# A decoder's forgetting attention with its gates added by TensorE in paired heads, and operand tiles of 258 columns

## The chip, the cores and the metric

The kernel runs on one core of a Trainium2 chip. The metric is the time of one launch on the device, in microseconds (us); lower is better. The kernel before takes 1029.21 us (median of 3 runs, 1028.37 to 1030.59).

A core has five engines, which run their own instruction streams: PE (matrix products; its weight loads are listed apart as PEld), DVE (vector work), ACT (activations), POOL, and SP, which here issues the DMAs. PE reads from the on-chip memory SBUF and writes PSUM.

## The reference

Two blocks of a decoder over 256 tokens of width 1024. The first mixes with a recurrent branch, gated linear attention and a block-sparse attention (MoBA), and ends in a SwiGLU feed-forward. The second has a short convolution layer, and a layer of forgetting attention (FoX), each with a SwiGLU feed-forward of width 2816. What the change touches is FoX, with 16 heads of 64:

```python
log_f = jax.nn.log_sigmoid((h @ w_f + b_f).astype(jnp.float32))
log_fcum = jnp.cumsum(log_f, axis=1).transpose(0, 2, 1)          # F, one row of 256 per head
logits = jnp.einsum("bhqd,bhkd->bhqk", qb, kb)                   # query blocks of 128
logits = logits + log_fcum[:, :, q0:kend, None] - log_fcum[:, :, None, :kend]
logits = jnp.where(kpos[None, :] <= qpos[:, None], logits, -jnp.inf)
p = jax.nn.softmax(logits, axis=-1)
outs.append(jnp.einsum("bhqk,bhkd->bhqd", p, vb))                # then o @ w_o
```

All other products are plain matrix products: activations times weight matrices.

## The kernel before, in words

Activations lie transposed: 128 features on the partitions, 256 tokens in the columns, 8 such tiles for the width. Every large product is made of three passes in the reduced format fp32r: an operand a is kept as a high part and a rest (`hilo`, `hl_tiles`), and a*w is computed as ah*wh + ah*wl + al*wh (`mm3`, L150 to L152; `ksteps`, L185 to L191). So a 128x128 weight block costs three matmuls of 256 columns. Weights stream from HBM as 512 KB chunks of 8 blocks (`raw`); ACT makes the high part of a chunk (L139, `wh`), DVE the rest (L143, `wl`). Beside them DVE computes a matrix-vector product of the modulation in pieces (`gw`, L359), spread over the program by `fill`.

The operands of the products are in three kinds of tiles, named by what they carry: `xh`/`xl`, `yh`/`yl` (both from `hl_tiles`, L244) and `mh`/`ml` (the feed-forward's inner operand, in `ffn`). Tiles of x are T + 2 = 258 columns wide, because in some stages two more columns are used; y and m tiles have 256. A tile of 258 fp32 columns has 1032 bytes on each partition, one of 256 has 1024, and tiles of a pool lie behind one another. The products that this concerns read columns 0 to 255 in either case.

FoX comes after the convolution layer's feed-forward. K is projected (`wk`), the gates' small projection and the log-sigmoid make F, V is projected (`wv`), and then a loop over 8 pairs of heads does for pair i: the query projection (`single("wq", i)`, 24 matmuls), for each head two logits products in fp32 (L691, L694) with a causal mask added by two bf16 products (L693, L696), DVE's addition of a bias tile with a maximum (L699, L700), ACT's exponentials (L703, L704), the scaling (L706, L707), three transposes by PE into a `plg` tile (L716 to L718), ACT's copy (L720), two products with V (L721, L722), and a step of the output projection `wo` (12 matmuls in `ksteps`). The bias F[t] - F[s] is brought to the 128 partitions through memory: F is written to a scratch row (`f_scr`, L1159), each pair reads its two rows back to all partitions (`f_b`, L1181), and ACT makes the bias tiles (`m_b`, L1186, L1187) from them and from a transposed copy of F.

The order on each engine is set when the program is built: a scheduler walks through the program with modelled times and lays down each engine's stream, and the engines then run in that order and wait on semaphores. `after` adds an order between two instructions.

Of the kernel before, what the change touches and what calls it, by code (L numbers as in the profile page):

```python
# [14 lines left out]
ALU = mybir.AluOpType  # L15
# [21 lines left out]
WARM = (5, 3, 5, 0)  # L37
RSQ_SEED = 1595953144
# [24 lines left out]
class Net:  # L63
# [180 lines left out]
    def hl_tiles(self, tag, pool=None):  # L244

        w = T + 2 if tag == "x" else T
        h = self.tl(pool or self.xp, [P, w], tag + "h", F32R, NK)
        l = self.tl(pool or self.xp, [P, w], tag + "l", F32R, NK)
        return h, l, h[:, 0:T], l[:, 0:T]
# [128 lines left out]
    def consts(self):  # L378
# [21 lines left out]
        nc.scalar.activation(self.tbl, self.tbl, AF.Exp)  # L400
        self.identb = self.tl(cp, [P, P], "identb", BF16)
# [281 lines left out]
    def attn_p(self, q, k, hh, bias, mask=False):  # L683
# [7 lines left out]
        mm(lg[:, 0:256], q[r, 128:256], k[r, 0:256], start=True, stop=not mask)  # L691
        if mask:
            mm(lg[:, 128:256], self.identb, self.cmask, start=False, stop=True)  # L693
        mm(lg[:, 256:384], q[r, 0:128], k[r, 0:128], start=True, stop=not mask)  # L694
        if mask:
            mm(lg[:, 256:384], self.identb, self.cmask, start=False, stop=True)  # L696
# [27 lines left out]
    def attn_out(self, i, Ls, v):  # L724
# [4 lines left out]
        return self.hilo(pv, "y")  # L729

# [49 lines left out]
    def ffn(self, l, X, R=None, R2=None, first=(), rows=None):  # L780
# [5 lines left out]
        def evac(g, u):  # L786
# [12 lines left out]
            h = self.tl(self.fp, [P, T], "mh", F32R)  # L799
            lo = self.tl(self.fp, [P, T], "ml", F32R)  # L800
# [151 lines left out]
    def run(self):  # L952
# [193 lines left out]
        fz = self.small_proj(1, XK)  # L1146
        z = self.tmp("f_z", bufs=1)[:32]
        A.activation(z, fz, AF.Copy)
        fz = self.ms([16, T])
        nc.tensor.matmul(fz, self.fold, z, start=True, stop=True)  # L1150
        z = z[:16]
# [210 lines left out]
```

## Time and profile before

| | us |
|---|---|
| median of 3 runs | 1029.21 |
| the profiled execution's own time | 1030.16 |
| its span (first to last instruction) | 1028.4 |
| PE busy | 956.9 (93%) |
| DVE busy | 810.7 (79%) |
| ACT busy | 537.0 (52%) |
| POOL busy | 20.5 (2%) |
[...]

Times in rows are us from the span's start unless ns stands beside them. [...] "[7.42 <-DVE a_mx L700]" behind a row is the idle time of the engine before that instruction, and what ended it. [...] The FoX loop stands at 706 to 798 us.

### The profile page before, as it was taken

The numbers are of one execution on the slowest core, as the hardware profiler recorded it, in microseconds if no ns is written. First come the engines' busy times: TensorE is split into PE (matmuls) and PEld (weight loads), VectorE is DVE, ScalarE is ACT, GpSimd is POOL, SyncE is SP. The second block draws the span as 40 slices with busy tenths as digits, with TensorE's granted clock in tenths as the row PEclk, the third lists the DMA queues.
The fourth block names the chain that finished last, engine by engine and source line by source line (L and its number), as shares of the span: only waits on it lengthen the run. The fifth ranks groups of instructions, "written<-read, shape, count | busy, mean of one in ns | idle before, by whom it ended". The sixth has DMA issues, their size and how long they took to land.

```text
span 1028.4 us, 19193 instructions
## 1 busy us (share of the span) xinstructions
PE 956.9 (93%) x7384; PEld 913.4 (89%) x7384; DVE 810.7 (79%) x1635; ACT 537.0 (52%) x971; POOL 20.5 (2%) x65
## 2 busy tenths in 40 slices
PE   7979998999999799987899999998899889999996
PEld 7878988999999699987899999977587889999995
DVE  7897487999887888779999999797355898866554
ACT  7575454544443544546454444486556575544432
POOL 1210000000000000000000000000000000000001
PEclk9999998999999899998899999999699989999998
DMA  8753256888899577654799999647332457565641
GB/s 302 252 169 106 83 187 209 281 296 282 294 334 369 182 232 247 197 169 177 262 323 340 315 335 374 189 131 243 99 122 86 124 160 234 181 186 184 185 141 41
DMA packets 63532, 221.69 MB, mean 216 GB/s; under 512 B 7256, under 2 KB 8944, under 8 KB 63440
## 3 DMA queue, kind: packets, MB, share of 16 engines
q1 hardware_dynamic: 62240, 217.18, 63.3%
q0 software_dynamic: 1056, 3.16, 1.1%
q8 instruction: 58, 0.95, 0.4%
q14 instruction: 34, 0.28, 0.1%
q10 hardware_dynamic: 144, 0.13, 0.0%
HBM read 219.36 MB, written 2.65 MB: 216 GB/s over the span
## 4 chain that ended last, share of the span: by engine, by line
PE 81%; DVE 11%; ACT 3%; issue 3%; DMA 2%; DVEq 0%; ACTq 0%; SPq 0%
PE acc L150 19%; PE acc L151 19%; PE acc L152 19%; PE acc L185 4%; PE acc L186 4%; PE acc L191 4%; DVE wl L143 3%; DVE gw L359 2%; PE ms L721 1%; ACT wh L139 1%; DMA f_b<-f_scr 1%; PE lg L691 1%; PE acc L241 1%; PE acc L240 1%; PE acc L239 1%
## 5 line engine op out<-in xcount | busy, mean ns | idle before, releaser
L139 ACT ACTIVATE wh<-raw 128x1024 fp32r<-128x1024 f32 (+2 forms) x296 | 307.5, 1046 | 272.4 <-PE acc L152 134.9
L143 DVE TENSOR_TENSOR wl<-raw,wh 128x1024 fp32r<-128x1024 f32 (+2 forms) x296 | 356.3, 1206 | 92.1 <-ACT wh L139 89.6
L150 PE MATMUL acc<-yh,wh 128*128 128x256 f32 x608 | 172.2, 284 | 0.7 <-DVE ff_m L798 0.7
L151 PE MATMUL acc<-yh,wl 128*128 128x256 f32 x608 | 172.3, 284 | 0.0
L152 PE MATMUL acc<-yl,wh 128*128 128x256 f32 x608 | 172.1, 284 | 0.0
L150 PE MATMUL acc<-xh,wh 128*128 128x256 f32 x576 | 164.1, 285 | 5.8 <-DVE ff_u L791 4.1
L151 PE MATMUL acc<-xh,wl 128*128 128x256 f32 x576 | 163.6, 284 | 0.0
L152 PE MATMUL acc<-xl,wh 128*128 128x256 f32 x576 | 163.2, 283 | 0.0
L151 PE MATMUL acc<-mh,wl 128*128 128x256 f32 x528 | 149.3, 283 | 0.5 <-DVE wl L143 0.5
L152 PE MATMUL acc<-ml,wh 128*128 128x256 f32 x528 | 149.1, 283 | 0.0
L150 PE MATMUL acc<-mh,wh 128*128 128x256 f32 x528 | 148.8, 283 | 0.0
L359 DVE SCALAR_TENSOR_TENSOR gw<-gw,cact 128x1024 f32<-128x1024 f32 x112 | 135.1, 1218 | 4.4 <-DMA gw<-ada 4.3
L150 PEld LDWEIGHTS acc<-yh,wh 128*128 128x128 f32 x608 | 116.9, 193 | 0.8 <-issue 0.8
L151 PEld LDWEIGHTS acc<-yh,wl 128*128 128x128 f32 x608 | 116.9, 192 | 0.0
L152 PEld LDWEIGHTS acc<-yl,wh 128*128 128x128 f32 x608 | 116.9, 192 | 0.0
L150 PEld LDWEIGHTS acc<-xh,wh 128*128 128x128 f32 x576 | 110.2, 191 | 6.9 <-DVE ff_u L791 4.3
L151 PEld LDWEIGHTS acc<-xh,wl 128*128 128x128 f32 x576 | 110.4, 192 | 0.6 <-issue 0.5
L152 PEld LDWEIGHTS acc<-xl,wh 128*128 128x128 f32 x576 | 110.0, 191 | 0.0
L151 PEld LDWEIGHTS acc<-mh,wl 128*128 128x128 f32 x528 | 101.4, 192 | 0.7 <-DVE wl L143 0.7
L152 PEld LDWEIGHTS acc<-ml,wh 128*128 128x128 f32 x528 | 101.3, 192 | 0.0
L150 PEld LDWEIGHTS acc<-mh,wh 128*128 128x128 f32 x528 | 101.1, 192 | 0.0
L185 PE MATMUL acc<-xh,wh 128*128 128x256 f32 (+1 forms) x256 | 68.3, 294 | 7.6 <-ACT wh L139 5.5
(382 smaller groups left out, 1604.7 us busy)
## 6 DMA issues: line engine op xcount, KB each, us to landing
raw<-wts SPq DMA_DIRECT2D x288, 512.0 KB, 4.4
gw<-ada SPq DMA_DIRECT2D x112, 512.0 KB, 5.4
f_b<-f_scr SPq DMA_DIRECT2D x8, 256.0 KB, 3.4
raw<-wts SPq DMA_DIRECT2D x6, 256.0 KB, 5.5
m_scr<-m_row POOLq DMA_DIRECT2D x2, 768.0 KB, 6.1
ax<-xT SPq DMA_DIRECT2D x4, 256.0 KB, 5.0
m_b<-m_scr POOLq DMA_DIRECT2D x8, 128.0 KB, 3.4
out<-fg SPq DMA_DIRECT2D x8, 128.0 KB, 1.8
```

What stands on the lines that cost most here:

```text
L139: i = nc.scalar.activation(self.wh[:, d], r, AF.Copy)
L143: self.anchor = nc.vector.tensor_tensor(self.wl[:, d], r, self.wh[:, d].bitcast(F32), ALU.subtract)
L150: m = [mm(ps, wh, xh, start=start, stop=False), mm(ps, wl, xh, start=False, stop=False), mm(ps, wh, xl, start=False, stop=stop)]
L151: mm(ps, wl, xh, start=False, stop=False),
L152: mm(ps, wh, xl, start=False, stop=stop)]
L185: m.append(mm(outs[i], wh, X[0][k], start=k == 0 and i % per == 0, stop=False))
L186: m.append(mm(outs[i], wl, X[0][k], start=False, stop=False))
L191: m.append(mm(outs[i], wh, X[1][k], start=False, stop=False))
L239: mm(outs[tt], h, wh, start=k == 0 and (tt == 0 or not one), stop=False)
L240: mm(outs[tt], l, wh, start=False, stop=False)
L241: mm(outs[tt], h, wl, start=False, stop=k == NK - 1 and (tt == 1 or not one))
L359: i = nc.vector.scalar_tensor_tensor(t, t, 1.0, self.cact, op0=ALU.mult, op1=ALU.mult, accum_out=self.ada[:, g:g + 1])
```

## The change

In words: (1) y and m tiles get 258 columns. (2) The gates' projection and log-sigmoid (`fox_gates`) are put ahead of the last quarter of K's projection, at high priority, and F is written three times as bf16 (a value and two rests) into rows 0 to 15, 32 to 47 and 64 to 79 of a tile G. (3) F[t] and -F[s] are added to the logits in PSUM by bf16 products over 80 rows of G with selectors (`fsel`, `fneg`), read with a repeated column; the scratch row, its read-backs and the bias tiles go. (4) The two heads of a pair, which lie on partitions 0 to 63 and 64 to 127, stand next to each other in the logits (`fox_logits`) and in the products with V (`fox_pv`). The maximum is taken by a plain reduction, negated, and ACT's exponential reads PSUM. Transposes go to `pms` tiles. (5) PE's order in the loop is the program's own (`manual_schedule`): query projection of pair i + 1, logits of pair i, transposes of pair i - 1, `wo` step of pair i - 2, products with V of pair i - 1.

```diff
-        w = T + 2 if tag == "x" else T
+        w = T + 2
...
+        nc.gpsimd.memset(self.G, 0.0)
+        self.fsel = self.tl(cp, [P, 16], "fsel", BF16)
+        nc.gpsimd.memset(self.fsel, 0.0)
+        for o in (0, 32, 64):
+            nc.vector.tensor_copy(self.fsel[o:o + 16, :], self.ident[o:o + 16, o:o + 16])
+        self.fneg = self.tl(cp, [P, 16], "fneg", BF16)
+        nc.vector.tensor_scalar(self.fneg, self.fsel, -1.0, None, ALU.mult)
         self.identb = self.tl(cp, [P, P], "identb", BF16)
         nc.vector.tensor_copy(self.identb, self.ident)
...
+    def fox_logits(self, i, q, k):
+
+        mm = self.nc.tensor.matmul
+        lg = [self.tl(self.plg, [P, 384], "lg") for _ in range(2)]
+        for o, w, t in ((0, T, slice(P, T)), (T, P, slice(0, P))):
+            for hh in range(2):
+                r = slice(64 * hh, 64 * hh + 64)
+                mm(lg[hh][:, o:o + w], q[r, t], k[r, 0:w], start=o == 0, stop=False)
+        G, n = self.G, G_ROWS
+        m = self.cmask.rearrange("p (a c) -> p a c", a=1).broadcast_to([P, 2, P])
+        for hh in range(2):
+            h = slice(2 * i + hh, 2 * i + hh + 1)
+            for o, w, t in ((0, T, slice(P, T)), (T, P, slice(0, P))):
+                mm(lg[hh][:, o:o + w], G[0:n, t], self.fsel[0:n, h].broadcast_to([n, w]), start=False, stop=False)
+                mm(lg[hh][:, o:o + w], self.fneg[0:n, h].broadcast_to([n, P]), G[0:n, 0:w], start=False, stop=False)
+            mm(lg[hh][:, P:384].rearrange("p (a c) -> p a c", a=2), self.identb, m, start=False, stop=True)
+        return lg
...
+    def fox_softmax(self, lg):
+
+        V, A = self.nc.vector, self.nc.scalar
+        mx = self.tmp("a_mx", (P, 4))
+        sm = self.tmp("a_sm", (P, 4))
+        Ls = [self.tmp("a_L", (P, 384), bufs=4) for _ in range(2)]
+        part = [(hh, j, s) for hh in range(2) for j, s in ((0, slice(0, T)), (1, slice(T, 384)))]
+        for hh, j, s in part:
+            c = slice(2 * hh + j, 2 * hh + j + 1)
+            V.tensor_reduce(mx[:, c], lg[hh][:, s], AX.X, ALU.max, negate=True)
+            A.activation(Ls[hh][:, s], lg[hh][:, s], AF.Exp, bias=mx[:, c], accum_out=sm[:, c])
+        V.reciprocal(sm, sm)
+        for hh, j, s in part:
+            V.tensor_scalar(Ls[hh][:, s], Ls[hh][:, s], sm[:, 2 * hh + j:2 * hh + j + 1], None, ALU.mult)
+        return Ls
...
+    def fox_pv(self, i, pts, v):
+
+        mm = self.nc.tensor.matmul
+        pv = self.ms([P, T])
+        vo = [64 * (2 * i + hh) for hh in range(2)]
+        for tt, o, p in ((0, 0, slice(0, 256)), (1, 128, slice(256, 384))):
+            for hh in range(2):
+                mm(pv[64 * hh:64 * hh + 64, o:T], v[tt][vo[hh] // T][:, vo[hh] % T:vo[hh] % T + 64], pts[hh][:, p],
+                   start=tt == 0, stop=tt == 1)
+        return self.hilo(pv, "y")
...
+    def fox_gates(self, fz):
+
+        nc = self.nc
+        V, A = nc.vector, nc.scalar
+        row = lambda tag, n=16: self.tmp(tag, bufs=1)[:n]
+        z = row("f_z", 32)
+        A.activation(z, fz, AF.Copy)
+        fz = self.ms([16, T])
+        nc.tensor.matmul(fz, self.fold, z, start=True, stop=True)
+        ab, z, y, ln, u = row("ls_a"), z[:16], row("ls_y"), row("ls_l"), row("ls_u")
+        A.activation(ab, fz, AF.Abs, bias=self.bf)
+        A.activation(z, fz, AF.Identity, bias=self.bf)
+        A.activation(y, ab, AF.Exp, scale=-1.0)
+        V.tensor_scalar(u, y, 1.0, None, ALU.add)
+        i = A.activation(ln, u, AF.Ln)
+        self.after(A.activation(self.tbl, self.tbl, AF.Exp), i)
+        V.scalar_tensor_tensor(ab, u, -1.0, y, op0=ALU.add, op1=ALU.subtract)
+        V.scalar_tensor_tensor(z, z, 0.0, ab, op0=ALU.min, op1=ALU.add)
+        F = self.tmp("f_F", (16, T), bufs=1)
+        V.tensor_tensor_scan(F, z, ln, 0.0, op0=ALU.add, op1=ALU.subtract)
+        G = self.G
+        for o in (0, 32, 64):
+            V.tensor_copy(G[o:o + 16, :], F)
+            if o < 64:
+                V.tensor_tensor(F, F, G[o:o + 16, :], ALU.subtract)
...
-            h = self.tl(self.fp, [P, T], "mh", F32R)
-            lo = self.tl(self.fp, [P, T], "ml", F32R)
+            h = self.tl(self.fp, [P, T + 2], "mh", F32R)[:, 0:T]
+            lo = self.tl(self.fp, [P, T + 2], "ml", F32R)[:, 0:T]
...
+        with self.tc.high_priority():
+            fz = self.small_proj(1, XK)
+            self.fox_gates(fz)
...
-        V.tensor_scalar(z, fz, self.bf, None, ALU.add)
-        lf = self.log_sigmoid(z, 16)
-        F = self.tmp("f_F", (16, T), bufs=1)
-        one = self.tmp("f_one", bufs=1)[:16]
-        G.memset(one, 1.0)
-        V.tensor_tensor_scan(F, one, lf, 0.0, op0=ALU.mult, op1=ALU.add)
-        fscr = self.tl(self.dp, [16, T], "f_scr")
-        nc.sync.dma_start(fscr, F)
-        fp = self.ms([P, 2, 16])
-        for tt in range(2):
-            nc.tensor.transpose(fp[:, tt, :], F[:, tt * P:tt * P + P], self.ident[:16, :16])
-        Fc = self.tl(self.cp, [P, 2, 16], "Fc")
-        V.tensor_copy(Fc, fp)
...
+        def wq(i):
             ps = self.single("wq", i, XQ, fill=i >= QF)
             q = self.tmp("a_q")
             A.activation(q, ps, AF.Copy, scale=0.125)
-            fb = self.tmp("f_b", (P, 2, T), bufs=2)
-            nc.sync.dma_start(fb, bass.AP(tensor=fscr.tensor, offset=fscr.offset + 2 * i * T, ap=[[0, P], [T, 2], [1, T]]))
-            Ls = []
-            for hh in range(2):
-                h = 2 * i + hh
-                B = self.tmp("m_b", (P, 384), bufs=3)
-                A.activation(B[:, 0:256], fb[:, hh, :], AF.Identity, scale=-1.0, bias=Fc[:, 1, h:h + 1])
-                A.activation(B[:, 256:384], fb[:, hh, 0:128], AF.Identity, scale=-1.0, bias=Fc[:, 0, h:h + 1])
-                Ls.append(self.attn_p(q, ks[i], hh, B, True))
-            if i == 1:
-                step, pre = self.partial("wo")
-            if i:
-                for j, t in enumerate(self.attn_out(i - 1, prev, vs)):
-                    Y[j].append(t)
+            return q
...
+        with self.tc.manual_schedule(engines={nc.tensor.engine}):
+            q = wq(0)
+            Ls = None
+            step, pre = self.partial("wo")
+            for i in range(NK + 1):
+                qn = wq(i + 1) if i < NK - 1 else None
+                lg = self.fox_logits(i, q, ks[i]) if i < NK else None
+                pts = self.fox_pt(Ls) if i else None
                 if i > 1:
                     step(Y, i - 2)
-            prev = Ls
-        step(Y, NK - 2)
-        for j, t in enumerate(self.attn_out(NK - 1, prev, vs)):
-            Y[j].append(t)
-        step(Y, NK - 1)
+                if i:
+                    out(i - 1, pts)
+                Ls = self.fox_softmax(lg) if i < NK else None
+                q = qn
+            step(Y, NK - 1)
```

PE at the logits of the second pair of heads (k is `f_k`, q is `a_q`; `lg` tiles hold a head's logits). Before:

```order
L691 MATMUL lg_9089<-f_k_8581,a_q_9082 128x256
L693 LDWEIGHTS identb_128
L693 MATMUL lg_9089<-cmask_130,identb_128 128x128
L694 MATMUL lg_9089<-f_k_8581,a_q_9082 128x128
L696 LDWEIGHTS identb_128
L696 MATMUL lg_9089<-cmask_130,identb_128 128x128
L691 MATMUL lg_9108<-f_k_8581,a_q_9082 128x256
L693 LDWEIGHTS identb_128
L693 MATMUL lg_9108<-cmask_130,identb_128 128x128
L694 MATMUL lg_9108<-f_k_8581,a_q_9082 128x128
L696 LDWEIGHTS identb_128
L696 MATMUL lg_9108<-cmask_130,identb_128 128x128
```

After, where the second head's eight rows of gates and mask come behind those of the first:

```order
L743 MATMUL lg_9121<-f_k_8590,a_q_9050 128x256
L743 MATMUL lg_9122<-f_k_8590,a_q_9050 128x256
L743 MATMUL lg_9121<-f_k_8590,a_q_9050 128x128
L743 MATMUL lg_9122<-f_k_8590,a_q_9050 128x128
L749 LDWEIGHTS fG_128
L749 MATMUL lg_9121<-fsel_130,fG_128 128x256
L750 LDWEIGHTS fneg_135
L750 MATMUL lg_9121<-fG_128,fneg_135 128x256
```

The two heads' products with q now follow each other, the masks between them are gone, and ten bf16 products (five a head) come behind.

PE at the transposes and the products with V of the first pair, after (before, each head's three transposes and its own two products stand by themselves, with other heads' work between):

```order
L775 MATMUL ms_9137<-ident_120,a_L_9070 128x128
L776 MATMUL ms_9137<-ident_120,a_L_9070 128x128
L777 MATMUL ms_9137<-ident_120,a_L_9070 128x128
L775 MATMUL ms_9143<-ident_120,a_L_9071 128x128
L776 MATMUL ms_9143<-ident_120,a_L_9071 128x128
L777 MATMUL ms_9143<-ident_120,a_L_9071 128x128
L790 MATMUL ms_9149<-a_pt_9141,fg_8963 64x256
L790 MATMUL ms_9149<-a_pt_9147,fg_8963 64x256
L790 MATMUL ms_9149<-a_pt_9141,fg_8967 64x128
L790 MATMUL ms_9149<-a_pt_9147,fg_8967 64x128
```

The four products with V, on different halves of the output rows, are next to each other.

DVE ahead of the loop, where F is made (`wl` and `gw` are weights and modulation). Before:

```order
L477 SCALAR_TENSOR_TENSOR ls_a_8788<-ls_u_8792,ls_y_8790 16x256
L478 TENSOR_TENSOR ls_l_8794<-ls_l_8794,ls_a_8788 16x256
L479 SCALAR_TENSOR_TENSOR f_z_8783<-f_z_8783,ls_l_8794 16x256
L143 TENSOR_TENSOR wl_9278<-raw_9275,wh_9277 128x1024
L1157 SCALAR_TENSOR_TENSOR f_F_8800<-f_one_8801,f_z_8783 16x256
L359 SCALAR_TENSOR_TENSOR gw_9293,ada_166<-gw_9293,cact_1819 128x1024
L143 TENSOR_TENSOR wl_9375<-raw_9372,wh_9374 128x1024
L359 SCALAR_TENSOR_TENSOR gw_9402,ada_166<-gw_9402,cact_1819 128x1024
L1164 COPY Fc_8809<-ms_8806 128x32
L143 TENSOR_TENSOR wl_9471<-raw_9468,wh_9470 128x1024
```

After:

```order
L811 SCALAR_TENSOR_TENSOR f_z_8642<-f_z_8642,ls_a_8646 16x256
L144 TENSOR_TENSOR wl_9179<-raw_9176,wh_9178 128x1024
L360 SCALAR_TENSOR_TENSOR gw_9206,ada_175<-gw_9206,cact_1828 128x1024
L813 SCALAR_TENSOR_TENSOR f_F_8658<-f_z_8642,ls_l_8648 16x256
L144 TENSOR_TENSOR wl_9242<-raw_9239,wh_9241 128x1024
L816 CAST fG_128<-f_F_8658 16x256
L818 TENSOR_TENSOR f_F_8658<-f_F_8658,fG_128 16x256
L816 CAST fG_128<-f_F_8658 16x256
L144 TENSOR_TENSOR wl_9299<-raw_9296,wh_9298 128x1024
L360 SCALAR_TENSOR_TENSOR gw_9314,ada_175<-gw_9314,cact_1828 128x1024
L818 TENSOR_TENSOR f_F_8658<-f_F_8658,fG_128 16x256
L816 CAST fG_128<-f_F_8658 16x256
```

The log-sigmoid is spread between the same `wl` and `gw` instructions, and five instructions on 16 rows that make G follow the running sum; no copy of F goes to memory.

## Rows read from the trace of the kernel before

**Rows 1.** The page's chain that ended last, shares of the span by engine.
```profile
PE 81%; DVE 11%; ACT 3%; issue 3%; DMA 2%; DVEq 0%; ACTq 0%; SPq 0%
```
**Rows 2.** Stretches of one core: length, busy time and number by engine, PEclk, DMA.
```profile
200.00:250.00 50.00, 50.00 (x428) 50.00 (x427) 47.29 (x84) 24.16 (x36) 0.00 (x0) 1.00 0.86 291
525.00:575.00 50.00, 50.00 (x419) 50.00 (x418) 46.93 (x85) 25.43 (x45) 0.00 (x0) 1.00 0.95 328
955.00:1005.00 50.00, 50.00 (x419) 50.00 (x418) 27.92 (x36) 19.97 (x23) 0.00 (x0) 1.00 0.50 153
```
**Rows 3.** Timeline of PE at the first logits that wait: start, us, instruction.
```profile
723.79 0.76 PE L691 MATMUL lg<-f_k,a_q 64*128 64x256 f32 x1 [7.42 <-DVE a_mx L700]
```
**Rows 4.** The chain in order of time at 712 to 722: start, us, what.
```profile
712.58 3.01 DMA f_scr<-f_F
715.64 6.74 DMA f_b<-f_scr
```
**Rows 5.** The stretch behind that wait, columns as in rows 2.
```profile
723.80:741.30 17.50, 16.48 (x51) 10.08 (x52) 7.35 (x44) 11.64 (x42) 0.00 (x0) 0.50 0.24 72
```
**Rows 6.** Timeline of PE, the last product with V in the loop.
```profile
797.62 0.38 PE L722 MATMUL ms<-a_pt,fg 128*64 128x128 f32 x2
```
**Rows 7.** PE's groups by form: names, shapes, count | busy us, mean ns | idle.
```profile
L150 PE MATMUL acc<-yh,wh 128*128 128x256 f32 x608 | 172.2, 284 | 0.7 <-DVE ff_m L798 0.7
...
L150 PE MATMUL acc<-mh,wh 128*128 128x256 f32 x528 | 148.8, 283 | 0.0
L185 PE MATMUL acc<-yh,wh 128*128 128x256 f32 x208 | 58.4, 308 | 16.1 <-ACT yh L254 12.5 <-DVE ff_g L932 2.7 <-DVE f_k L932 0.9
```
**Rows 8.** Timeline of DVE from the end of the operand work on.
```profile
695.74 1.22 DVE L143 TENSOR_TENSOR wl<-raw,wh 128x1024 fp32r<-128x1024 f32 x1
...
701.36 1.21 DVE L359 SCALAR_TENSOR_TENSOR gw<-gw,cact 128x1024 f32<-128x1024 f32 x1
...
706.83 0.41 DVE L477 SCALAR_TENSOR_TENSOR ls_a<-ls_u,ls_y 16x256 f32<-16x256 f32 x1
```
**Rows 9.** Timeline of PE in the first block's attention, two heads side by side.
```profile
92.92 0.71 PE L691 MATMUL lg<-a_k,a_q 64*128 64x256 f32 x4
...
93.78 0.39 PE L150 MATMUL acc<-xh,wh 128*128 128x256 f32 x1
```
**Rows 10.** Timeline of PE in FoX, one head's logits and masks.
```profile
769.47 0.23 PE L693 MATMUL lg<-cmask,identb 128*128 128x128 bf16 x1
769.63 0.48 PE L694 MATMUL lg<-f_k,a_q 64*128 64x128 f32 x2
770.05 0.23 PE L696 MATMUL lg<-cmask,identb 128*128 128x128 bf16 x1
770.09 0.36 PE L150 MATMUL acc<-xh,wh 128*128 128x256 f32 x1
```
**Rows 11.** Timeline of PE in FoX, one head's transposes.
```profile
753.48 0.27 PE L716 MATMUL lg<-ident,a_L 128*128 128x128 f32 x1
...
753.70 0.27 PE L718 MATMUL lg<-ident,a_L 128*128 128x128 f32 x1
```
**Rows 12.** Timeline of PE in the first block's attention, products with V.
```profile
100.28 0.66 PE L721 MATMUL ms<-a_pt,fg 128*64 128x256 f32 x4
...
101.09 0.39 PE L185 MATMUL acc<-yh,wh 128*128 128x256 f32 x1
```
**Rows 13.** DVE's groups by form in 706 to 798.
```profile
L699 DVE CUSTOM_DVE_ANT_0 a_L<-lg,m_b 128x256 f32<-128x256 f32 x16 | 6.8, 422 | 19.4 <-PE lg L696 15.3 <-ACT m_b L1186 3.9
```
**Rows 14.** ACT's groups by form in the same stretch.
```profile
L139 ACT ACTIVATE wh<-raw 128x1024 fp32r<-128x1024 f32 x11 | 11.6, 1052 | 3.4 <-PE acc L191 3.3
...
L703 ACT ACTIVATE a_L<-a_L,a_mx 128x256 f32<-128x256 f32 x16 | 7.9, 496 | 0.3 <-DVE a_mx L701 0.3
L720 ACT ACTIVATE a_pt<-lg 128x384 f32<-128x384 f32 x16 | 7.7, 480 | 3.1 <-PE lg L718 2.9
```
**Rows 15.** Timeline of DVE at the start of the program.
```profile
4.27 0.20 DVE L569 COPY g_z<-vec 128x2 f32<-128x2 f32 x1 [1.61 <-DMA vec<-vec]
```

More of the change, by code (lines that the diff above doesn't have):

```diff
@@ L37 @@
 WARM = (5, 3, 5, 0)
+G_ROWS = 80
 RSQ_SEED = 1595953144
@@ L681, in gla, with attn_p @@
         return out
-    def attn_p(self, q, k, hh, bias, mask=False):
+    def attn_p(self, q, k, hh, bias):
         nc = self.nc
@@ L690, in attn_p @@
         mm = nc.tensor.matmul
[L691 to L696, printed above, removed]
+        mm(lg[:, 0:256], q[r, 128:256], k[r, 0:256], start=True, stop=True)
+        mm(lg[:, 256:384], q[r, 0:128], k[r, 0:128], start=True, stop=True)
         L = self.tmp("a_L", (P, 384), bufs=4)
@@ new lines, in fox_pt @@
+    def fox_pt(self, Ls):
+        out = []
+        for L in Ls:
+            tp = self.ms([P, 384])
+            self.nc.tensor.transpose(tp[:, 0:128], L[:, 256:384], self.ident)
+            self.nc.tensor.transpose(tp[:, 128:256], L[:, 0:128], self.ident)
+            self.nc.tensor.transpose(tp[:, 256:384], L[:, 128:256], self.ident)
+            pt = self.tmp("a_pt", (P, 384))
+            self.nc.scalar.activation(pt, tp, AF.Copy)
+            out.append(pt)
+        return out
+    def fox_pv(self, i, pts, v):
[7 more added lines that the diff above has]
+        return self.hilo(pv, "y")
@@ L1175, in run @@
         Y = ([], [])
-        for i in range(NK):
+        def wq(i):
             ps = self.single("wq", i, XQ, fill=i >= QF)
@@ L1179, in run, with out @@
             A.activation(q, ps, AF.Copy, scale=0.125)
-            fb = self.tmp("f_b", (P, 2, T), bufs=2)
-            nc.sync.dma_start(fb, bass.AP(tensor=fscr.tensor, offset=fscr.offset + 2 * i * T, ap=[[0, P], [T, 2], [1, T]]))
-            Ls = []
-            for hh in range(2):
-                h = 2 * i + hh
-                B = self.tmp("m_b", (P, 384), bufs=3)
-                A.activation(B[:, 0:256], fb[:, hh, :], AF.Identity, scale=-1.0, bias=Fc[:, 1, h:h + 1])
-                A.activation(B[:, 256:384], fb[:, hh, 0:128], AF.Identity, scale=-1.0, bias=Fc[:, 0, h:h + 1])
-                Ls.append(self.attn_p(q, ks[i], hh, B, True))
-            if i == 1:
-                step, pre = self.partial("wo")
-            if i:
-                for j, t in enumerate(self.attn_out(i - 1, prev, vs)):
-                    Y[j].append(t)
+            return q
+        def out(i, pts):
+            for j, t in enumerate(self.fox_pv(i, pts, vs)):
+                Y[j].append(t)
+        with self.tc.manual_schedule(engines={nc.tensor.engine}):
[6 more added lines that the diff above has]
+                pts = self.fox_pt(Ls) if i else None
                 if i > 1:
                     step(Y, i - 2)
-            prev = Ls
-        step(Y, NK - 2)
-        for j, t in enumerate(self.attn_out(NK - 1, prev, vs)):
-            Y[j].append(t)
-        step(Y, NK - 1)
+                if i:
[3 more added lines that the diff above has]
+            step(Y, NK - 1)
         self.close()
```

7 lines of the change are left out of this document (1 added, 6 removed).

## The prediction

> **What bounds the kernel now.** First the page's chain that ended last: PE holds 81% of it and DMA 2% [rows 1], so the end moves if matmuls come closer together or if PE stops waiting. The second thing read is therefore the spacing of matmuls in streams without gaps, by stretches of 50 us [rows 2]. All three stretches stand at full granted clock with PE busy for the whole of it, and their matmuls have the same form, 256 columns of fp32r. The first (x tiles, 258 columns wide) holds 428 of them, 50000 / 428 = 116.8 ns each; the other two (y tiles, then m tiles, 256 wide) hold 419, 119.3 ns each. The difference is 2.5 ns. The third is the timeline of PE around the FoX loop. Its largest gap is 7.42 us before 723.79, at logits that wait for the first pair's softmax [rows 3]. The chain in order of time says what the softmax waited for: the scratch write at 712.58 and the read-back, which landed at 715.64 + 6.74 = 722.4 [rows 4]. [...] The loop's last product with V ends at 797.62 + 0.38 = 798.0 [rows 6].
>
> **Part 1: wider y and m tiles.** Nothing is added on any engine; what changes is where the tiles begin. Is it the tile that makes the 2.5 ns, or the stage? In rows 2 the two 256-wide stretches differ widely in everything else (DMA share 0.95 against 0.50, DVE busy 46.9 against 27.9 us) and have the same 419; the x stretch has DVE and DMA loads like the first of them and 428. So load is no explanation, and the tile's width or place is the only difference that I see. The products on such tiles are, by groups with three passes each [rows 7], (608 + 208 + 528) x 3 = 4032. Of them 192 (`wo`, counted in part 2 and behind it) and 48 (two columns of `wk`, among waits) I leave out: 3792 x 2.5 ns = 9.5 us, all on PE's path in streams. Bounds: 0 (it is not the tile) and 10.1 us (all 4032). I take 9.5. DVE, at 94% in the busiest of these stretches, would go to 96%, so it still hides.
>
> [...]
>
> **Part 2: the FoX loop.** Here I rebuild PE's work, since its order is now written out, and then add waits.
>
> The start. Pair 0 needs G. From 695.74 on DVE has, in the order printed above and just ahead of it, eight `wl` (1.22), four `gw` (1.21) and nine instructions on 16 rows at about 0.41 until G is complete [rows 8]: 9.8 + 4.8 + 3.7 = 18.3, plus 0.3 of hand-overs, so 714.3. PE has done the first two query projections by then and waits a little. No DMA is in this path any more: the scratch write, the eight read-backs on SP's queue, the 32 bias activations on ACT (L1186, L1187) and the transposed copy go, and SP's queue holds only weights and modulation.
>
> One pair on PE:
> - query projection: 24 x 117.5 ns = 2.82 us (x tiles, rows 2, a little above 116.8 for the switches).
> - products with q: in the first block's attention two heads' logits stand side by side, and the four products, two passes each, take 93.78 - 92.92 = 0.86 us for both heads [rows 9]. In FoX before, each head was alone.
> - gates and mask: ten bf16 products, four of 128 columns and six of 256; the trace has none over 80 rows. The nearest are the two masks of 128 columns: the one between two products of 64 rows costs 769.63 - 769.47 = 0.16, the one that a full-height product follows 770.09 - 770.05 = 0.04 [rows 10]. [...] In the new order the ten stand behind one another, which is nearer to the second row: 1.2. [...]
> - transposes: 0.11 apart [rows 11], six are 0.66.
> - `wo` step: 12 x 117.5 = 1.41.
> - products with V of both heads, side by side: 101.09 - 100.28 = 0.81 [rows 12].
> Sum 7.76 a pair, eight pairs 62.1. The last `wo` step stands behind the last product with V (-1.41), and six matmuls of the next stage are moved in ahead of it (+0.7): 61.4. Of these the first two query projections and the first products with q (5.64 + 0.86) are over before G is. From 714.3 on there remain 54.9.
>
> The waits. After its logits a pair needs a reduction (0.42, by L699), four exponentials of up to 0.50, four scalings that I put at the reduction's 0.42 too, and an estimated 0.7 of hand-overs and a reciprocal before it can be transposed [rows 13, 14]: 4.8 us. Between a pair's logits and its transposes PE now has the previous pair's transposes, a `wo` step, products with V, a query projection and the next logits: 0.66 + 1.41 + 0.81 + 2.82 + 2.06 = 7.8. So in the middle the chain is covered, with 3.0 us to spare for one `wl` on DVE and one `wh` (1.05) on ACT between its links. Not covered: the copy of the first transposes, where no `wo` step stands between (two copies of 0.48 [rows 14], 1.0), the second pair's logits, which need both `lg` tiles (0.5), and the last transposes, which have only 2.9 us in front of them (1.8). For ACT being busy with a `wh` when a copy is due I take 0.5 in each of six pairs, 3.0. Together 6.3. The last product with V ends at 714.3 + 54.9 + 6.3 = 775.5 against 798.0: 22.5 us earlier. Behind it the last `wo` step waits for `hilo` of the last pair, which before lay under other work: 0.9 back. Part 2 gives 21.6. It holds the gap of 7.4 and what the half clock cost: with no gap of that length I expect no fall of the clock in the loop.
>
> **Part 3: the start of the program.** Four small DVE instructions and two POOL memsets more stand ahead of the first weights. DVE waits there 1.61 us for a transfer anyway, which ends at 4.27 [rows 15], and that hides them; what of the reordering reaches behind it I put at 0.3 us, some two of the 0.20 instructions that stand there.
>
> **The sum.** -9.5 - 21.6 + 0.3 = -30.8 us. Against the profiled execution's own 1030.16 that is 999.4; it ran 0.95 above the median of 1029.21, and against the median the forecast is 998.4 us. Taking the bounds: gates at 1.9 add 5.6, no waits and gates at 0.85 take off 9.1, part 1 at nothing adds 9.5.
>
> **The rivals.**
> - *Tiles do nothing.* x stages differ from the others in something else that I don't see. Against it: rows 2, three stretches with two counts. Time 998.4 + 9.5 = 1007.9.
> - *PE's fixed order waits.* Before, the scheduler put other matmuls in front of a late softmax; now PE stands behind it. If ACT's and DVE's weight chunks come in front of two links in each pair, a pair waits 2 us in place of 0.8: 8 x 2 = 16 against 6.3, time 1008. For it: `wh` and `wl` take over 1 us each [rows 8, 14]. Against it: the 3.0 us to spare.
> - *No waits and cheap gates.* 998.4 - 9.1 = 989.3.
> - *Slower: the waits bring the clock down and hold it there.* The place is the FoX loop. [...] If waits in every pair keep the loop at 0.50, its 55 us of work double, +55, and the time is 1053. It decides from the point at which the work done at half clock, which costs its own length again, passes the 30.8 won: 31 of 55 us. Against it: at 7.76 of work and 0.8 of waits a pair, the order leaves PE 90% filled.
>
> **How the numbers follow.** Forecast 0.64 (its own range 992 to 1004); tiles do nothing 0.12; order waits 0.12; no waits 0.07; slower by the clock 0.03; the change doing nothing at all on balance 0.02. The range 988 to 1011 holds the first four cases nearly whole. A change of under 0.2%, 2 us, can't be told from none here: faster 0.95, same 0.01, slower 0.04.
>
> **What would show it.** Part 1 is right if stretches of y and m hold about 428 matmuls in 50 us, as x does; wrong if 419 stay. Part 2: no DMA in the chain before the loop, no gap of several us at the first logits, PEclk 1.00 from there to the end of the loop, four products with q or V in under 0.9 us, a pair in 7.8 to 8.6 us, the last product with V about 22 us nearer to the end of V's projection than before. The pair is wrong if PE's idle time before transposes or products with V names ACT or DVE in most pairs. The whole is wrong above 1011, first of all if PEclk falls in the loop.

## The result, and the profile after

The changed kernel takes 1001.05 us (median of 4 runs, 1000.39 to 1001.65) against 1029.04 of the kernel before in the same runs: ratio 0.9726, 95% interval 0.9709 to 0.9743. The forecast was 998.4. The profiled span falls from 1028.45 to 999.86. By stages, cut at the first and last 258-column product of the three `lazy` stretches, whose starts stand in both traces:

| stage | before | after | won |
|---|---|---|---|
| start to the end of the first `lazy` | 459.55 | 457.31 | 2.24 |
| feed-forward, its down product, second `lazy` | 209.93 | 207.61 | 2.32 |
| FoX, to the first product of the third `lazy` | 139.58 | 117.83 | 21.75 |
| third `lazy` | 22.86 | 23.00 | -0.14 |
| last feed-forward to the end | 196.53 | 194.11 | 2.42 |

The chain that ended last, which answers to [rows 1]:

```profile
PE 78%; DVE 13%; issue 4%; ACT 3%; DMA 1%; POOL 0%; DVEq 0%; ACTq 0%; POOLq 0%
```

The three streams of [rows 2] (x, y, m tiles; length, busy us and number by engine, PEclk, which is the clock that PE was granted as a share of its full one, DMA):

```profile
200.00:250.00 50.00, 50.00 (x428) 50.00 (x427) 47.30 (x85) 24.77 (x36) 0.00 (x0) 1.00 0.85 292
515.00:565.00 50.00, 50.00 (x428) 50.00 (x427) 47.84 (x89) 26.07 (x47) 0.00 (x0) 1.00 0.95 337
925.00:975.00 50.00, 50.00 (x423) 50.00 (x422) 28.05 (x36) 20.94 (x24) 0.00 (x0) 1.00 0.50 158
```

The second line went from 419 to 428, as forecast; the third only to 423. From starts of all products of a stream: x 117.5 ns before and after, y 120.0 to 117.7, m 120.0 to 118.9. (Here and below a spacing is the mean distance from start to start, distances over 135 ns left out. A product's own time is longer, 284 ns in the mean of the y products [rows 7] that start 120.0 apart: products overlap, and what one costs in a stream is the distance.)

In the FoX loop the gap of [rows 3] is 4.17 us, and what ends it is DVE, not a transfer: the last rest of F goes to G at 710.68.

```profile
711.02 0.28 PE L749 MATMUL lg<-fsel,fG 80*128 80x256 bf16 x1 [4.17 <-DVE fG L816]
```

DVE's timeline ahead of it, where chunks of weights and of the modulation stand between the links:

```profile
705.04 0.67 DVE L813 TENSOR_TENSOR_SCAN f_F<-f_z,ls_l 16x256 f32<-16x256 f32 x1
705.65 1.19 DVE L144 TENSOR_TENSOR wl<-raw,wh 128x1024 fp32r<-128x1024 f32 x1
...
707.83 1.23 DVE L144 TENSOR_TENSOR wl<-raw,wh 128x1024 fp32r<-128x1024 f32 x1
708.97 1.22 DVE L360 SCALAR_TENSOR_TENSOR gw<-gw,cact 128x1024 f32<-128x1024 f32 x1
...
710.68 0.28 DVE L816 CAST fG<-f_F 16x256 bf16<-16x256 f32 x1
```

Behind the gap the granted clock is 0.50 for 3.4 us, against 17.5 in [rows 5]; then it stands at 1.00 to the loop's end. Products of 256 columns start 0.214 us apart in it (712.68 to 714.82) and 0.117 behind it (715.22 to 715.92), so at 0.50 one costs 1.8 times as much:

```profile
711.80:715.20 3.40, 3.40 (x19) 3.40 (x17) 2.32 (x9) 1.93 (x8) 0.00 (x0) 0.50 0.62 224
720.00:740.00 20.00, 20.00 (x176) 17.82 (x173) 13.65 (x39) 11.95 (x37) 0.00 (x0) 1.00 0.39 124
```

One pair in the middle of the loop, on PE (start, duration, instruction):

```profile
738.86 0.92 PE L743 MATMUL lg<-f_k,a_q 64*128 64x256 f32 x8
739.72 0.28 PE L749 MATMUL lg<-fsel,fG 80*128 80x256 bf16 x1
...
740.61 0.27 PE L775 MATMUL ms<-ident,a_L 128*128 128x128 f32 x1
...
741.19 0.36 PE L186 MATMUL acc<-yh,wh 128*128 128x256 f32 x1
...
742.75 0.87 PE L790 MATMUL ms<-a_pt,fg 128*64 128x256 f32 x8
743.55 0.38 PE L151 MATMUL acc<-xh,wh 128*128 128x256 f32 x1
```

Start to start: products with q 0.86, gates and masks 0.89, transposes 0.58, `wo` step 1.56, products with V 0.80; the query projection behind it lasts to 746.56, 3.01. Sum 7.70, with no wait in it.

### The profile page after: what moved, and what is told of

It reads as the page before. It is cut to its first block, busy times and chain, and to the rows that moved or that the text cites. A ratio compares the mean times of both kernels' runs of the same rounds, so it can differ in the third digit from the quotient of the medians.

```text
span 999.9 us, 19159 instructions
## 1 busy us (share of the span) xinstructions
PE 933.7 (93%) x7430; PEld 900.9 (90%) x7430; DVE 809.8 (81%) x1584; ACT 525.7 (53%) x941; POOL 20.3 (2%) x66
## 3 DMA queue, kind: packets, MB, share of 16 engines
q0 software_dynamic: 1056, 3.16, 1.1%
## 4 chain that ended last, share of the span: by engine, by line
PE 78%; DVE 13%; issue 4%; ACT 3%; DMA 1%; POOL 0%; DVEq 0%; ACTq 0%; POOLq 0%
PE acc L151 19%; PE acc L153 19%; PE acc L152 18%; PE acc L186 4%; PE acc L187 4%; DVE wl L144 4%; PE acc L192 4%; DVE gw L360 3%; ACT wh L140 1%; PE ms L790 1%; DMA gw<-ada 1%; PE acc L189 1%; PE lg L743 1%; DVE yl L256 1%; PE acc L242 1%
## 5 line engine op out<-in xcount | busy, mean ns | idle before, releaser
L152 PE MATMUL acc<-yh,wl 128*128 128x256 f32 x608 | 170.2, 280 | 0.0
L151 PEld LDWEIGHTS acc<-yh,wh 128*128 128x128 f32 x608 | 114.7, 189 | 0.9 <-issue 0.9
L152 PEld LDWEIGHTS acc<-yh,wl 128*128 128x128 f32 x608 | 114.8, 189 | 0.4 <-issue 0.4
L153 PEld LDWEIGHTS acc<-yl,wh 128*128 128x128 f32 x608 | 114.5, 188 | 0.6 <-issue 0.6
L152 PEld LDWEIGHTS acc<-mh,wl 128*128 128x128 f32 x528 | 99.4, 188 | 0.7 <-DVE wl L144 0.7
L151 PEld LDWEIGHTS acc<-mh,wh 128*128 128x128 f32 x528 | 99.1, 188 | 0.0
```

The costliest lines, as they stand in the source:

```text
L151: m = [mm(ps, wh, xh, start=start, stop=False), mm(ps, wl, xh, start=False, stop=False), mm(ps, wh, xl, start=False, stop=stop)]
L152: mm(ps, wl, xh, start=False, stop=False),
L153: mm(ps, wh, xl, start=False, stop=stop)]
```

## Experiments

All ratios are to the kernel before, timed beside the run. "Place" is the start of a tile on its partition modulo 256 bytes, from the addresses that the compiled program gives its tiles; these lie at multiples of 32. In the kernel before, all y and m tiles and all weight tiles lie at place 160. In the changed kernel the weights lie at 96, and x, y and m tiles, 1056 bytes apart, at all eight places in turn.

### The tiles

**e1: the tiles alone.** The kernel before with the two edits on tile widths.

```diff
-        w = T + 2 if tag == "x" else T
+        w = T + 2
-            h = self.tl(self.fp, [P, T], "mh", F32R)
+            h = self.tl(self.fp, [P, T + 2], "mh", F32R)[:, 0:T]
```

> The kernel before, with y and m tiles 258 columns wide and nothing else changed. By the two traces: y products 117.5 ns apart in place of 120.0, m products 118.9 in place of 120.0, together about -6.9 us, so 1022. By the prediction (2.5 ns on all of them): -9.5, so 1019.7. By a rule in which the spacing depends on the column count alone: 0, 1029. If the two parts of the change help one another, this and the FoX part alone do not add up to -28.

1028.26 us, ratio 0.9976 (0.9959 to 0.9992); 1022 was expected from the spacing. The streams read as in the changed kernel (y 117.7, m 118.9), and the stages outside FoX win 2.9, 2.2 and 2.6 us. But FoX takes 143.4 in place of 139.6, with 23.9 us at half clock behind its gap and 6.8 more later, and the third `lazy` 24.6 in place of 22.9:

```profile
714.40:738.30 23.90, 18.31 (x60) 11.92 (x61) 8.61 (x49) 13.47 (x46) 0.00 (x0) 0.50 0.33 109
```

So the spacing is the tiles' doing, the forecast of the time failed, and the parts don't add up. In the old loop most of what the streams win is given back at half clock: 30.7 us of the FoX stretch stand there, against 23.9 in the kernel before. Half of the 6.8 us more is 3.4 of the 3.8 us that it lost, an estimate: by the 0.214 and 0.117 us above a little under half of the time at 0.50 is lost.

**e2: the FoX part alone.** The changed kernel without those edits.

> The changed kernel with y and m tiles 256 columns wide again, as before. By the two traces: y and m products 120.0 ns apart again, though all these tiles now begin 96 B past a multiple of 256 B (160 in the kernel before), since a common place costs the same wherever it is; 6.9 us over the changed kernel, 1008. By the prediction 1010.5. If the place itself (160) and not its being common made the 120.0, the spacing is another one here.

1008.79 us, ratio 0.9784 (0.9762 to 0.9805). y and m stand at 120.0, now at place 96 with the weights at 96; the y stream:

```profile
515.00:565.00 50.00, 50.00 (x419) 50.00 (x418) 47.48 (x89) 26.03 (x46) 0.00 (x0) 1.00 0.95 333
```

Its span is 6.7 us longer than the changed kernel's: that is part 1 beside the new loop. FoX takes 118.9 here, so of the 21.75 us won there 20.7 are the loop's own and 1.1 the tiles'.

**e3: wide, but all alike.**

```diff
-        w = T + 2
+        w = T + 2 if tag == "x" else T + 64
```

> The changed kernel with y tiles 320 columns wide in place of 258, so that successive y tiles are 1280 B apart, five times 256, and again all begin at the same place modulo 256 B. Theory 'step of place' (spacing = 120 ns + 7.5 ns for each 32 B by which the next moving tile begins later modulo 256 B, not under about 109): y products back at 120.0 ns, about 4.6 us over the changed kernel, 1005.6. Theory 'any width over 256 helps': 117.5, no change, 1001.

1007.63 us, ratio 0.977 (0.9749 to 0.9792); y at 120.0, where 258 columns gave 117.7. Width is not what matters. The formula in this expectation, "120 + 7.5 ns for each 32 B of step" with its floor, is an estimate from the two traces, where it met all fourteen streams of x, y and m within 0.5 ns. The x streams, with a step of -32 B in one product of three, read 117.5, so that step stands at 112.5; m, mostly with steps of 0, -64 and 32 B, reads 118.9, so -64 B stands at 3 x 118.9 - 120 - 127.5 = 109.2, the floor, and not at 105. The next run was to test it.

**e4: another order in a column.** The passes of `single` and `pair` sorted, for eight k-steps at a time.

```diff
-        for k in range(nk):
-            self.mm3(t, wname, k, c, X[0][k], X[1][k], k == 0, k == nk - 1)
+            ws = [self.weights(wname, k, c)[:2] for k in ks]
+            todo = [(ws[k - k0][a], X[b][k]) for a, b in ((0, 0), (0, 1), (1, 0)) for k in ks]
```

> The changed kernel with the three passes of a column in another order: eight k-steps of the high weights with the high tiles, then eight with the low tiles, then eight of the low weights with the high tiles, in place of three passes for each k-step; same matmuls, same sum but for its order. So nearly every matmul moves 32 B down modulo 256 B from the one ahead, in place of one in three. Theory 'step of place': x, y and m products of these columns 112.5 ns apart in place of 117.5 to 118.9; over all such products 780.6 us become 754.5, so up to -26 us, 975, less where DVE or DMA then bounds a stretch. Theory 'width': 117.5 stays, 1001. A rule of the column count alone: 1001.

997.2 us, ratio 0.9669 (0.9647 to 0.9691), but not for that reason. With a step of -32 B at most products the spacing is 117.8 to 118.1 in all streams, where the formula gave 112.5 to some 115:

```profile
200.00:250.00 50.00, 50.00 (x427) 50.00 (x426) 46.82 (x85) 25.45 (x36) 0.00 (x0) 1.00 0.87 290
515.00:565.00 50.00, 50.00 (x427) 50.00 (x426) 47.37 (x89) 24.97 (x45) 0.00 (x0) 1.00 0.94 334
925.00:975.00 50.00, 50.00 (x427) 50.00 (x426) 28.54 (x38) 19.89 (x23) 0.00 (x0) 1.00 0.47 144
```

The step is refuted. The streams visit the same eight places as in the changed kernel, about equally often, in another order. The 3.8 us that the span is shorter than the changed kernel's come out of the last stage, 190.1 us in place of 194.1, where PE idles 2.4 us less, and in smaller parts out of the others; FoX takes 3.4 us more.

**e5 and e9: one place at a time.** y and m 256 wide (in e9 also x, at 320), with spare bytes ahead, so that each stream has one place.

```diff
+        self.tl(self.xp, [P, 40], "pad", F32, 1)
...
+        w = (1, 2, 3)[l]
+        self.tl(self.fp, [P, 8 * w], "pad", F32, 1)
```

> The changed kernel with y and m tiles 256 columns wide, and spare bytes ahead of them, so that all y tiles begin at 0 modulo 256 B and the m tiles of the three FFNs at three other places (32, 64 and 96). Theory 'common place' (where all tiles begin alike the spacing is 120.0 ns, whatever the place): y and m 120.0, 1008 as with the FoX part alone. Theory 'place modulo 64 B' (the 120.0 belongs to tiles that begin 32 B past a multiple of 64, which is where 160 and 96 lie): 120.0 for m at 32 and 96, and 115 for y at 0 and for m at 64, since the tiles of x, half of which begin on a multiple of 64, stand at 117.5 on average; y alone would then give 2400 x 5 ns = 12 us, 996.

1002.88 us, ratio 0.9726 (0.9708 to 0.9745). Neither theory: m at place 32 reads 114.7, at 64 118.3, at 96 120.0; y at 0 reads 118.7 in one feed-forward and 117.6 in the other, with the same place and the same distance to the weights, so that 1.1 ns hang on something else, which stays open. The y stream that reads 118.7 and the m stream at 96:

```profile
515.00:565.00 50.00, 50.00 (x423) 50.00 (x423) 47.45 (x90) 26.33 (x47) 0.00 (x0) 1.00 0.94 338
...
930.00:980.00 50.00, 50.00 (x419) 50.00 (x418) 28.36 (x38) 19.32 (x23) 0.00 (x0) 1.00 0.46 144
```

> As the run before with common places, at the places not yet seen: y tiles all at 160 modulo 256 B, the m tiles of the three FFNs at 128, 192 and 224, and x tiles (320 columns wide, so that they too begin alike) all at 32. The weight tiles begin at 96, as in every variant of the changed kernel; in the kernel before they began at 160, with all y and m tiles at 160 too. Theory 'place against the weights' (120.0 belongs to tiles that begin where the weights begin): y at 160 is 64 B off the weights and leaves 120.0, as m at 32 did with 114.7 at 64 B off on the other side; x at 32 reads 114.7 in place of 117.5, which alone gives 2600 x 2.8 ns = 7.3 us. Theory 'place in memory' (160 and 96 are bad of themselves): y stays at 120.0; x at 32 reads 114.7 as well. Theory 'common place': 120.0 everywhere, 1014 or so.

995.14 us, ratio 0.9658 (0.9624 to 0.9692). x at place 32 reads 113.4. y at 160 reads 117.8 with the weights at 96, where it read 120.0 with the weights at 160 before. The x, y and two of the m streams:

```profile
200.00:250.00 50.00, 50.00 (x443) 50.00 (x442) 48.41 (x86) 25.84 (x39) 0.00 (x0) 1.00 0.87 301
...
515.00:565.00 50.00, 50.00 (x427) 50.00 (x426) 47.74 (x88) 25.65 (x46) 0.00 (x0) 1.00 0.94 331
585.00:635.00 50.00, 50.00 (x419) 50.00 (x419) 45.80 (x72) 23.21 (x32) 0.00 (x0) 1.00 0.96 350
920.00:970.00 50.00, 50.00 (x424) 50.00 (x423) 28.65 (x36) 19.98 (x23) 0.00 (x0) 1.00 0.49 157
```

By place of the moving tile less place of the weights:

| bytes | -96 | -64 | -32 | 0 | 32 | 64 | 96 | 128 |
|---|---|---|---|---|---|---|---|---|
| ns | 117.6, 118.7 | 113.4, 114.7 | 118.3 | 120.0 | 116.7 | 117.8 | 120.0 | 118.7 |
| read from | y, e5 | x, e9; m, e5 | m, e5 | before, e2, e3, e5 | m, e9 | y, e9 | m, e9 | m, e9 |

The mean over the eight, with the mean where there are two, is 118.0, and e4's streams stand near it. But that the streams of mixed places are such a mean is not shown. The starts and the addresses allow it to be read product by product in the changed kernel. Where one tile meets several weights in a row (x tiles, as in `ksteps`), the table comes back within 0.8 ns: 119.5 at distance 0, 118.2 at -32, 118.8 at -96, 117.0 at 64, 120.1 at 96, 119.0 at 128; only -64 reads 117.5. Where tiles at different distances follow each other, as in `single` and `pair`, a product (its start to the next one's) does not stand at the value of its own distance: x and y products read 117.3 at 0 and 115.5 at 96, and in e4 121.8 at 64 and 115.9 at -64. So the neighbours count too, in a way that these runs don't settle.

**e11: the weights moved.** 64 bytes ahead of the weights put them at 160; all x, y and m tiles go to 96, the place that gave 120.0 in e2, e3 and e5 (by widths and spare bytes as in e9, left out here).

```diff
+        self.tl(cp, [P, 16], "padw")
```

> The changed kernel with 64 spare bytes ahead of the weight tiles, so that these begin at 160 modulo 256 B in place of 96, and with all x (320 columns wide), y and m tiles (256 wide) at 96, that is 64 B below the weights. In two earlier runs tiles at 96 with weights at 96 stood at 120.0 ns. Theory 'place against the weights': 113.4 (as x at 32 with weights at 96) to 114.7 (as m there) in all three kinds. From the 995.1 of the run before, 2400 y products x 4.3 and 1584 m products x 3.7 ns give 979, up to 990 where DVE or DMA bounds a stretch. Theory 'place in memory': 120.0 in all three kinds as for y and m at 96 before, and x slower by 2.4, 1014.

987.84 us, ratio 0.959 (0.9558 to 0.9622). The long streams fall to 113.3 to 114.2; where one y tile meets several weights in a row, 117.2 is left. The y and the last m stream:

```profile
515.00:565.00 50.00, 50.00 (x443) 50.00 (x442) 49.42 (x91) 25.78 (x39) 0.00 (x0) 1.00 0.97 351
...
905.00:955.00 50.00, 50.00 (x444) 50.00 (x443) 29.62 (x38) 20.90 (x25) 0.00 (x0) 1.00 0.53 159
```

The same place reads 120.0 with weights at 96 and 113.3 with weights at 160, so it is not the place itself but the distance to the weights that decides, or to something that moved with them: `raw`, `gw` and the later constants shift by the same 64 bytes, and no run tells them apart. The six runs spread over 978.6 to 992.5, and the trace is of the fastest; DVE and the transfers are nearly full in the y stretch (49.42 of 50 us, 0.97), and whether these set the rest of the time wasn't tried.

### The FoX loop

The stretch of FoX, from one profiled execution of each kernel; "clock" is half of the time that stood at 0.50, an estimate of what that cost (by 0.214 and 0.117 us for a product a little under half), "idle" PE's idle time, "work" what is left:

| kernel | length | clock | idle | work |
|---|---|---|---|---|
| before | 139.6 | 12.0 | 11.8 | 115.8 |
| e1, tiles alone | 143.4 | 15.4 | 12.9 | 115.2 |
| changed | 117.8 | 3.4 | 7.8 | 106.6 |
| e7, gates early | 141.0 | 17.1 | 9.1 | 114.9 |
| e10, gates by products | 125.6 | 3.4 | 6.3 | 115.9 |
| e8, written order, no pairs | 126.0 | 3.4 | 8.5 | 114.1 |
| e6, pairs, no written order | 122.7 | 3.4 | 6.2 | 113.1 |

The table leaves out the third `lazy` behind the stretch: it takes 22.9 us before, 23.0 in the changed kernel and in e6, but 24.4 to 25.0 in e1, e7, e8, e10 and e12, where PE idles some 1.5 us longer in it.

**e6: the scheduler's order.**

```diff
-        with self.tc.manual_schedule(engines={nc.tensor.engine}):
+        if True:
```

> The changed kernel with PE's order in the FoX loop left to the scheduler in place of written out; gates, pairs and tiles as in the changed kernel. Theory 'gates': what was won in the loop came from the gap and the half clock that went with the transfers, and from cheap gates, so the order is worth little: 1001 to 1004. Theory 'order': without it the pairs' chains collide with other work and PE waits in each pair, 1 us each: 1009 or more. Theory 'fixed order waits' (a rival of the prediction): the scheduler fills waits, under 1000.

1004.72 us, ratio 0.9746 (0.9727 to 0.9765). PE idles less, as "fixed order waits" has it, but works 6.5 us longer. The loop has 32 products with V and 32 with q, each of two passes (in the rows of one pair under the result, x8 is four of them). From start to next start, with waits taken off, those with V go up from 8.1 to 12.0 us, those with q from 6.9 to 10.2: the scheduler puts other products between the two heads in seven of eight pairs with V and in three with q, and some of both stand in the half clock. In the time of the whole kernel the order is worth less, 2 us by the ratios (0.9746 against 0.9726, with overlapping intervals).

**e7: the gates early, nothing else.** The old gate block, moved.

```diff
+        with self.tc.high_priority():
+            fz = self.small_proj(1, XK)
...
+            nc.sync.dma_start(fscr, F)
```

> The kernel before with one thing changed: the gates' projection, log-sigmoid, scan and scratch write stand ahead of the last two columns of wk at high priority, as in the changed kernel, while the read-backs, the bias on ACT, the single heads and the narrow tiles stay. Theory 'gap and clock': the 7.4 us gap and the half clock behind it (17.5 us with 51 matmuls, some 8.7 us lost) go, 1013 to 1016. Theory 'pairs and cheap gates': the gap was covered by little else than it cost, the loop stays bound by its 16 single heads; 1024 to 1029.

1030.0 us, ratio 0.999 (0.9977 to 1.0003). The gap of [rows 3] falls from 7.42 to 1.86 us, and nothing is won: the half clock comes all the same, for as long, and 10.2 us more of it stand later in the loop, at 775.6.

```profile
719.95 0.67 PE L691 MATMUL lg<-f_k,a_q 64*128 64x256 f32 x2 [1.86 <-DVE a_mx L700]
```

The stretch behind it, columns as in [rows 2]:

```profile
721.00:738.00 17.00, 14.51 (x47) 8.72 (x47) 7.49 (x37) 11.72 (x41) 0.00 (x0) 0.50 0.33 121
```

By the timeline most of these 47 are products of single heads, with waits for the softmax between them; ahead of the rise at 738 stand full-height products of 256 columns without a gap, 0.21 us apart from 735.82 on. So a fall of the clock doesn't need the long gap, and "gap and clock" is refuted: without it nothing came back.

**e8: no pairs.** The two loops over the heads put outside.

```diff
-        for o, w, t in ((0, T, slice(P, T)), (T, P, slice(0, P))):
-            for hh in range(2):
+        for hh in range(2):
+            for o, w, t in ((0, T, slice(P, T)), (T, P, slice(0, P))):
```

> The changed kernel with the two heads of a pair one behind the other in the products with q and with V, in place of side by side. In the trace of before one head's four products with q take about 0.8 us and its four with V 0.79; side by side both heads take 0.86 and 0.81 in the changed kernel. Theory 'pairs': 0.75 us for each of the two kinds, 1.5 a pair, 12 us, 1013. Theory 'hidden': PE waits for softmax anyway, 1001 to 1004.

1010.99 us, ratio 0.9806 (0.9789 to 0.9824); FoX loses 8 us of the 12 expected. The products with q cost 7.5 us more, 14.4 in place of 6.9. Those with V cost no more (7.7 and 8.1): the order of the program keeps them dense, not the alternation. PE's groups with q and V in the changed kernel (count | busy us, mean ns):

```profile
L790 PE MATMUL ms<-a_pt,fg 128*64 128x256 f32 x32 | 6.9, 405 | 0.3 <-ACT a_pt L779 0.3
L743 PE MATMUL lg<-f_k,a_q 64*128 64x256 f32 x32 | 5.6, 428 | 0.0
```
The same of e8:

```profile
L746 PE MATMUL lg<-f_k,a_q 64*128 64x256 f32 x32 | 11.7, 446 | 0.0
...
L789 PE MATMUL ms<-a_pt,fg 128*64 128x256 f32 x32 | 6.3, 404 | 0.3 <-ACT a_pt L778 0.3
```

**e10: only the gates by products.** The edits of e6 and e8 together, so the wide tiles stay too.

> The changed kernel with the heads of a pair one behind the other and PE's order left to the scheduler: of the FoX edits only the gates by products are left, with the wide tiles. Before, the stretch from the second lazy block to the third took 139.6 us, in the changed kernel 117.8; without the written order 122.7, without pairs 126.0. Theory 'sum of its parts': 117.8 + 4.9 + 8.1 = 130.8, so 1014, and the gates are worth 9 us. Theory 'the order only keeps pairs together': without pairs it is worth nothing, 126, 1009, and the gates 13.6. Theory 'the clock': without pairs and order the half clock comes back as in the kernel before (24 us of it there, 12 lost), 138 or more, 1021.

1009.56 us, ratio 0.9788 (0.976 to 0.9817); FoX 125.6. "The order only keeps pairs together" holds: without pairs it is worth nothing. So of the 21.75 us the gates by products, with the softmax that goes with them and the wide tiles, carry 14.0 (8.5 of it clock, 5.5 idle time), pairs and order together 7.8 (9.3 of work, less 1.5 of idle time). Against e1, which has the wide tiles too, the gates are worth 17.8. Why the half clock ends after 6.8 us here, with single heads, and lasts 17.1 in e7 is narrowed down to what the two differ in: the gates by products with their softmax, the transposes to `pms` tiles, the order in which the loop is written, and the wide tiles, which by themselves (e1) don't shorten it. It is narrowed down no further.

### A version that beats both

**e12.** All moving tiles at 32, weights at 96 (by widths and spare bytes, left out here), and a query projection more ahead of the first logits.

```diff
-            q = wq(0)
+            q = [wq(0), wq(1)]
...
-                qn = wq(i + 1) if i < NK - 1 else None
+                if i < NK - 2:
+                    q.append(wq(i + 2))
```

> The changed kernel with all x, y and m tiles at 32 and the weights at 96, again 64 B apart, and in the FoX loop the query projection of the third pair put ahead of the first pair's logits (each projection one pair earlier). Tiles: as in the run before by 'place against the weights', 979 to 990; by 'place in memory' 113.4 to 114.7 too, since 32 was read so. Loop: PE waits 4.2 us for the gates at the first logits, and 24 products of 117.5 ns, 2.8 us, now stand in that wait; theory 'cover': the wait falls to 1.4 and the run is 3 us under the tiles alone. Theory 'weights first': the third projection's weight chunks go through DVE ahead of the gates, these come later by as much, and nothing is won.

980.36 us (974.96 to 982.47), ratio 0.9504 (0.948 to 0.9528). The long streams stand at 113.3 to 113.6. FoX takes 114.4, 3.5 us less than in e11 (1.6 of which the third `lazy` gives back, 25.0 against 23.4), as "cover" has it, but by another sum: the wait falls by 1.3 us only, since G comes 1.2 later against V's projection, and the half clock behind it is 3.4 us in place of 6.8. Both traces are of the fastest run of their kernel.

```profile
693.82 0.28 PE L756 MATMUL lg<-fsel,fG 80*128 80x256 bf16 x1 [2.98 <-DVE fG L823]
```

## Why the prediction was right, and where it was off

**Part 1, -9.5 forecast, -7.0 measured.** The -7.0 are the stages outside FoX; e2 gives 6.7 in all. The step held that the tiles make the 2.5 ns, and e1 and e2 show it. The term that was mis-sized is the one price for all: y won 2.3 to 2.4 ns, m 1.1. 1584 m products x 1.4 ns are 2.2 us of the missing 2.5. I had taken x's spacing for a property of wide tiles; it belongs to tiles that come at eight distances to the weights, and one distance kept gives 113.3 to 120.0 (e5, e9, e11). Why m, on the same eight places, stands at 118.9 in the changed order and at 117.9 in e4's stays open.

The same count of columns takes 113.3 to 120.0 ns in these runs, so the count alone does not set the spacing. With the m tiles at one place and the weights moved by 64 bytes, m products go from 120.0 to 113.3 (e2, e11), by the weights or by what moved with them.

**Part 2, -21.6 forecast, -21.75 measured.** The sum hit by luck, with errors that cancel; without the tiles' 1.1 us in this stretch (e2) it is -20.7.
- Start: G was put at 714.3 in the old kernel's times; it is complete at 710.96, which with the 4.56 us that the stages ahead have won is 715.5.
- The pair: 7.76 forecast, 7.70 measured. The gates were too dear: 1.2 was put between 0.85 and 1.9, two ends that rest on a time for each column that no run shows; the ten take 0.89 here, with starts 0.11 to 0.12 us apart behind 256 columns and 0.05 to 0.06 behind 128. The projection and the `wo` step were too cheap by 0.2 each: at a switch between kinds of products the starts are 0.20 to 0.22 us apart in this pair, against 0.11 to 0.12 within the projection and the step.
- The waits: 6.3 forecast. From G to the last product with V PE has 0.9 us of waits (0.25, 0.28, 0.33) and loses some 1.7 to the half clock (half of its 3.4, an estimate). So 6.3 was 3.7 too dear. But some 20 products of the next stage stand ahead of the last product with V, not 6, 1.8 us more at 117.7 ns, and another 1.7 us of work are put down to no term. So the span from G to the end is 61.0 us, where 54.9 + 6.3 = 61.2 was forecast.
- "With no gap of that length I expect no fall of the clock" is the weak step. There was a gap of 4.2 us and a short fall, and e7 shows that a long fall comes without the long gap too.

**Part 3, +0.3**, can't be told apart from the rest of the first stage; nothing speaks against it.

**The rivals.** "Tiles do nothing" fell with e1 (y from 120.0 to 117.7) and e2 (back at 120.0). "PE's fixed order waits" is true of the idle time (7.8 against 6.2 in e6) and false of the sum, since the order keeps the heads together. "No waits and cheap gates" was near in both its parts (0.9 us of waits, gates at 0.89) and still missed the time by 12 us, since part 1 won 2.5 us less, G came 1.2 later, and the half clock and the work named above stand in none of its terms. The slower rival, half clock through the loop with its work doubled, did not come in the changed kernel, where a product at 0.50 costs 1.8 times as much; in e1, where the stretch stands 30.7 us at half clock, most of the tiles' gain goes that way.

## What to carry over

Where a stream's spacing is off by a few per cent at full clock, look at where the moving tiles and the weights begin, not only at counts and loads: in this kernel the tiles' places were worth more (14 us between the changed kernel's ratio and e11's) than pairs and order (7.8). A formula that meets every stream of two traces isn't yet tested, if all its variation comes from one layout; one run in which it must give a number never seen (112.5) showed that it was wrong. And ask of each part what it is worth beside the others: the tiles win 2 us in the old loop and 7 in the new one.

## What was not expected of the hardware

- fp32r products of 256 columns at full clock stand 113.3 to 120.0 ns apart, by the distance of the moving tile's start from the weights' modulo 256 bytes, where a stream keeps one distance (e2, e3, e5, e9, e11); lowest at -64, highest at 0 and 96.
- Two heads side by side on partitions 0 to 63 and 64 to 127 take 6.9 us for 32 fp32 products (64 passes) over 64 rows, one after the other 14.4 (e8); for products with 64 output rows (with V) the order of the heads makes next to no difference (8.1 and 7.7).
- Ten bf16 products over 80 rows, operands with a repeated column among them, cost 0.89 us in the changed kernel; at the 117.5 ns that 256 columns take in streams of x, their 2048 columns would take 0.94 (an estimate), so the repeated column costs nothing that shows.
